# First layer of a two-block model on one Trainium2 core: TensorE's order around the state-space quarters written by hand, attention gate and bias rows moved into it

## Chip, core and metric

The kernel runs on one core of one Trainium2 chip. Five engines each work through a queue of their own: TensorE (PE in the profile, its weight loads PEld), VectorE (DVE), ScalarE (ACT), GpSimd (POOL) and SyncE (SP, which here only issues DMAs). The metric is the device time of one execution in microseconds.

## What is computed

`x` of 1024 tokens by 1024 goes through an even layer (sliding-window attention beside a state-space model), an odd layer (attention over selected tokens) and a second block. The change touches the even layer alone:

```python
def even_layer(hn, rel_bias, w_in, w_out, q_g, k_g, sinks, log_dt, a_re, a_im, b_re, b_im,
               c_re, c_im, d_skip, glu_w, glu_b):
...
    q, k, v, gate_a, u, gate_b = split_cols(hn @ w_in, EVEN_SPLITS)
    q = rms_norm(q.reshape(bsz, L, A_HEADS, A_HEAD_DIM), q_g)
    k = rms_norm(k.reshape(bsz, L, A_KV_HEADS, A_HEAD_DIM), k_g)
...
    att = swa_sink_attention(q, k, v, sinks, rel_bias) * jax.nn.silu(gate_a)
    ssm = s5_mixer(u, log_dt, a_re, a_im, b_re, b_im, c_re, c_im, d_skip, glu_w, glu_b) * jax.nn.silu(gate_b)
    return jnp.concatenate([att, ssm], axis=-1) @ w_out
```

`EVEN_SPLITS` is 512 columns of q, 128 of k, 128 of v, 512 of `gate_a`, 512 of `u` and 512 of `gate_b`. `s5_mixer` projects `u` into 32 groups of 64 complex states, runs a linear recurrence over the tokens, projects back, applies gelu and a gated linear layer.

## The kernel before, in words

**Products.** Every weight product is made in three matmuls (lines 148 to 150): both operands are split into a high and a low part, and high by high, high by low and low by high are added in PSUM. One *step* below is one such group of three. `form1` takes 128 tokens as stationary operand and streams 512 or 256 weight columns; `form2` takes 128 weight columns and streams 512 tokens. A product over the 1024 input features is 8 steps into one PSUM bank of tag `mm`, of which there are 3.

**Weights.** `wpiece` (line 105) loads 128 by 512 from memory (SP's queue), copies it as the high part on ACT (line 122) and subtracts on POOL for the low part (line 123). 13 such tiles fit.

**The first layer, `phase_a` (line 268).** The tokens are normalised and transposed into `hnTA`. Then `bias_rows` makes four small matmuls (`brp`) that turn the position table into rows in memory. The columns `u` are multiplied out (8 banks) and stored. The state-space model works in 4 quarters of 8 groups. `setup(q)` transposes the output table (`craw` to `sg`), forms the tables `w2`, `m3`, `E` on DVE and POOL, multiplies `psG` (stored to `d_g` in 8 DMAs), and transposes `w2` into `m2` through `psm`. All of `sg`, `psG`, `psm` and `brp` use one PSUM bank of tag `sg`. `main(q)` loads its part of `u`, transposes it (`psu`), multiplies by `m2` (`psinc`), and then DVE makes a complex product `z`, eight scans over the tokens and a second complex product `x`. Beside this 16 DMAs load `m1` from `d_g`. `psy` adds `m1` by `u` and `m3` by `x`; DVE copies `y`, `psyT` transposes it, ACT applies gelu.

**Filler.** The products of q (8 banks of 512 columns), of k and v (8 banks of 256) and of `gate_b` (8 banks, `form2`) follow in the program text. A scheduler that works from the dependences and estimated times decides where each instruction stands on its engine; it mixes these products between the quarters' small matmuls. After each bank of q or k, `head_norm` (line 389) squares on ACT, reduces and multiplies on DVE from PSUM into a tile `qo` (tag `qo`, 2 slots, which the bias rows' tiles use too) and stores it to `d_qkv` from SP. After the quarters the PSUM banks are given out anew, and `gate_a` is multiplied out (64 steps), with ACT writing silu of it straight into the tile `mixA`. Then come the gated linear layer `GluA` (which loads `d_gb` into `mixA2`, line 715), the attention `SWA` and the output tiles.

**Names in the rows.** `mm<-w,hnTA` is a product of `form1`, `mm<-hnTA,w` one of `form2`, `mm<-yTs,w` one of the gated linear layer; `zr`, `zi`, `xr`, `xi` are DVE's complex products, `tv` its scratch tile.

## Time and profile before

| what | us |
|---|---|
| median of 3 runs | 2110.9 (2109.47 to 2115.68) |
| the profiled execution, its own time | 2114.89 |
| its span | 2112.6 |

The profiled execution's granted TensorE clock is 0.958 of full speed on average. A row of the timeline gives the start from the beginning of the span, the duration, the engine, the line and the operation; in square brackets stands how long the engine had been idle and what ended this. A row of the stretches gives the stretch, its length, the busy time of PE, PEld, DVE, ACT and POOL (each with its instructions), the granted clock as a share of 2.4 GHz, the busy share of the DMA engines and GB/s. Matmuls overlap in the pipeline, so the time that one costs is read from the distance of two starts.

### The profile page before, as it was taken

Reading aid. Unit: us, or ns where it says so; the run is one execution under the profiler, and the core shown is the slowest. Engines: PE = TensorE matmul, PEld = TensorE weight load, DVE = VectorE, ACT = ScalarE, POOL = GpSimd, SP = SyncE. Lnnn points to the kernel's source line nnn. Section 1 sums busy time; section 2 is a strip of 40 time slices with the busy share of each in tenths; the row PEclk is TensorE's granted clock in tenths of the full one; section 3 lists DMA queues with packets and bytes.
Section 4 is the critical chain, followed back from the end, with each engine's and each line's share of the span. In section 5 each row is a group of like instructions: output and inputs, shape, how many; then the busy total and the mean of one; then the engine's idle time right before and its main releaser. Section 6 shows DMA issues by size and latency. Waiting matters only on the chain. (4 is left out here: it accounts for less than half of the span.)

```text
span 2112.6 us, 27651 instructions
## 1 busy us (share of the span) xinstructions
PE 1938.3 (92%) x9291; PEld 1569.1 (74%) x9291; DVE 1505.6 (71%) x2947; ACT 857.7 (41%) x1740; POOL 920.6 (44%) x774
## 2 busy tenths in 40 slices
PE   7988899989999998899989999999999659999998
PEld 6777777777888876677767788788888537778786
DVE  8375513584469988688856399999997488857737
ACT  5222326564456896555546111223322411134210
POOL 5567416545322247565547221222232586643204
PEclk9989989999999999899999999999999869999999
DMA  6543332313212212643345232223333445575442
GB/s 199 157 121 100 117 125 83 115 49 101 90 56 75 71 46 83 190 171 122 123 150 190 81 103 68 69 90 95 124 118 102 154 136 164 175 243 175 159 160 100
DMA packets 165671, 256.19 MB, mean 121 GB/s; under 512 B 29078, under 2 KB 77548, under 8 KB 165530
## 3 DMA queue, kind: packets, MB, share of 16 engines
q1 hardware_dynamic: 154026, 232.43, 34.6%
q10 hardware_dynamic: 10224, 17.82, 2.3%
q0 software_dynamic: 1280, 4.20, 0.5%
q8 instruction: 73, 1.20, 0.2%
q14 instruction: 68, 0.56, 0.1%
HBM read 185.35 MB, written 75.06 MB: 123 GB/s over the span
## 5 line engine op out<-in xcount | busy, mean ns | idle before, releaser
L123 POOL TENSOR_TENSOR w<-wraw,w 128x512 fp32r<-128x512 f32 (+1 forms) x230 | 312.8, 1374 | 664.6 <-ACT w L122 660.5
L1289 DVE SCALAR_TENSOR_TENSOR cy<-u,cw,cy 128x1024 f32<-128x1024 f32 x232 | 298.7, 1287 | 5.7
L122 ACT ACTIVATE w<-wraw 128x512 fp32r<-128x512 f32 (+1 forms) x230 | 141.2, 623 | 189.6 <-DMA wraw<-in_w_in_dram 47.7
L149 PE MATMUL mm<-hnTC,w 128*128 128x512 f32 (+1 forms) x336 | 131.6, 392 | 0.0
L150 PE MATMUL mm<-hnTC,w 128*128 128x512 f32 (+1 forms) x336 | 131.5, 391 | 0.0
L148 PE MATMUL mm<-hnTC,w 128*128 128x512 f32 (+1 forms) x336 | 131.5, 391 | 0.0
L1167 POOL TENSOR_TENSOR lgB<-lgB,sc 128x1024 f32<-128x1024 f32 (+5 forms) x48 | 84.4, 1791 | 71.7 <-DMA lgB<-d_T 56.6
L148 PE MATMUL mm<-w,ms 128*128 128x512 f32 x256 | 106.0, 414 | 9.7 <-ACT ms L1021 9.3
L150 PE MATMUL mm<-w,ms 128*128 128x512 f32 x256 | 106.5, 416 | 4.3 <-POOL ms L1022 4.2
L1078 ACT ACTIVATE tkj<-sc,tks 128x896 bf16<-128x896 f32 (+2 forms) x93 | 96.7, 1042 | 22.2 <-DVE tks L1074 19.5
L149 PE MATMUL mm<-w,ms 128*128 128x512 f32 x256 | 103.9, 406 | 1.8 <-DVE w L120 1.0
L148 PE MATMUL mm<-w,hnTB 128*128 128x512 f32 x192 | 78.4, 409 | 11.0 <-ACT qo L401 7.7
L148 PE MATMUL mm<-w,hnTA 128*128 128x512 f32 (+1 forms) x192 | 73.4, 386 | 7.6 <-DVE qo L415 7.6
L148 PE MATMUL mm<-hnTB,w 128*128 128x512 f32 (+2 forms) x208 | 79.1, 380 | 0.5 <-DVE wit L872 0.5
L149 PE MATMUL mm<-hnTB,w 128*128 128x512 f32 (+2 forms) x208 | 78.8, 379 | 0.0
L150 PE MATMUL mm<-hnTB,w 128*128 128x512 f32 (+2 forms) x208 | 78.8, 379 | 0.0
L150 PE MATMUL mm<-w,hnTB 128*128 128x512 f32 x192 | 76.9, 400 | 0.0
L149 PE MATMUL mm<-w,hnTB 128*128 128x512 f32 x192 | 76.4, 401 | 0.0
L150 PE MATMUL mm<-w,hnTA 128*128 128x512 f32 (+1 forms) x192 | 73.5, 384 | 0.0
L149 PE MATMUL mm<-w,hnTA 128*128 128x512 f32 (+1 forms) x192 | 72.8, 380 | 0.3 <-POOL w L123 0.3
L148 PEld LDWEIGHTS mm<-hnTC,w 128*128 128x128 f32 (+1 forms) x336 | 61.6, 183 | 14.5
L150 PEld LDWEIGHTS mm<-hnTC,w 128*128 128x128 f32 (+1 forms) x336 | 61.6, 183 | 14.4
(611 smaller groups left out, 5895.1 us busy)
## 6 DMA issues: line engine op xcount, KB each, us to landing
wraw<-in_w_in_dram SPq DMA_DIRECT2D x56, 256.0 KB
wraw<-in_od_w_in_dram SPq DMA_DIRECT2D x48, 256.0 KB
wraw<-in_ev_w_in_dram SPq DMA_DIRECT2D x32, 256.0 KB
wraw<-in_w_in_dram SPq DMA_DIRECT2D x64, 128.0 KB
wraw<-in_w_out_dram SPq DMA_DIRECT2D x32, 256.0 KB
ld<-d_cs SPq DMA_DIRECT2D x16, 512.0 KB
hr<-h SPq DMA_DIRECT2D x24, 256.0 KB
d_T<-d_row SPq DMA_DIRECT2D x8, 576.0 KB
```

The costliest lines, as they stand in the source:

```text
L122: nc.scalar.activation(t[:, 0, :o], raw[:, :o], AF.Copy)
L123: nc.gpsimd.tensor_tensor(t[:, 1, :o], raw[:, :o], t[:, 0, :o].bitcast(F32), op=ALU.subtract)
L148: mm(out, aH, bH, start=start, stop=False)
L149: mm(out, aH, bL, start=False, stop=False)
L150: self.last = mm(out, aL, bH, start=False, stop=stop)
L1078: S.activation(self.junk(n), sc[b], AF.Sign, bias=cand[:, i:i + 1], accum_out=cnt[:, i:i + 1])
L1167: G.tensor_tensor(lg[:, :n], lg[:, :n], self.masks[b], op=ALU.add)
L1289: V.scalar_tensor_tensor(py if i < 30 else y, u[:, i:i + L], cw[:, ct, i:i + 1], py, op0=ALU.mult, op1=ALU.add)
```

## The change

What it does, part by part. (1) TensorE's order around the quarters is written out by hand (`manual_schedule`): `setup` and `main` become generators that stop at fixed places, `filling` yields after every step of q, k and v, `gate_b` and `gate_a` (for k and v after two steps of 256 columns), and `take(n)` issues n of them. In each quarter: 3, `psu`, 4, `psinc`, the next quarter's table transposes and load of `u`, 24, `psy`, 5, `psyT`, 4, `psG` and `psm` of the next quarter. The last call takes what is left. The other engines stay with the scheduler. (2) The bias rows are made one at a time, 4 steps ahead of each. (3) `gate_a` goes into the filler; its silu goes to memory (`d_ga`) in 8 stores of ACT and comes back into `mixA` by 4 loads of 512 KB on SP. (4) `m3` and `E` have 4 slots in place of 3 (two sets). (5) `head_norm` of q, k has ACT copy PSUM into `qo` first and works from there. (6) To make room, the norm's `gb` and `jk` use slots of `m1` and `uT`, and the state-space pools are opened earlier.

```diff
+    def steps1(self, out, hnT, tok0, wt, nk, w):
+
+        for k in range(nk):
+            self.mm3(out, hnT[:, 0, k, tok0:tok0 + P], hnT[:, 1, k, tok0:tok0 + P],
+                     wt[k][:, 0, :w], wt[k][:, 1, :w], k == 0, k == nk - 1)
+            yield
+
+    def steps2(self, out, hnT, tok0, wt, nk, m0):
+
+        for k in range(nk):
+            self.mm3(out, wt[k][:, 0, m0:m0 + P], wt[k][:, 1, m0:m0 + P],
+                     hnT[:, 0, k, tok0:tok0 + 512], hnT[:, 1, k, tok0:tok0 + 512], k == 0, k == nk - 1)
+            yield
+
...
         nc.scalar.dma_start(k.d_row[:, i * 384:(i + 1) * 384], row)
+        yield
...
+    def filling():
         wq = k.wchunk(W, 0, 512)
         for tt in range(NT):
             ps = k.mm()
-            k.form1(ps, hnT, tt * P, wq, KT, 512)
-            head_norm(k, xp, ps, 8, 64, d_qkv[tt * P:(tt + 1) * P, 0:512])
+            yield from k.steps1(ps, hnT, tt * P, wq, KT, 512)
+            head_norm(k, xp, ps, 8, 64, d_qkv[tt * P:(tt + 1) * P, 0:512], 2)
         wkv = k.wchunk(W, 512, 256)
         for tt in range(NT):
             ps = k.mm()
-            k.form1(ps[:, :256], hnT, tt * P, wkv, KT, 256)
+            for i, _ in enumerate(k.steps1(ps[:, :256], hnT, tt * P, wkv, KT, 256)):
+                if i % 2:
+                    yield
             vt = xp.tile([P, 128], F32, tag="vt", name="vt")
             S.activation(vt, ps[:, 128:256], AF.Copy)
             nc.scalar.dma_start(d_qkv[tt * P:(tt + 1) * P, 640:768], vt)
-            head_norm(k, xp, ps[:, :128], 2, 64, d_qkv[tt * P:(tt + 1) * P, 512:640])
-        wg = k.wchunk(W, 1792, 512)
-        for m in range(4):
-            for th in range(2):
-                ps = k.mm()
-                k.form2(ps, hnT, th * 512, wg, KT, m * P)
-                gt = xp.tile([P, 512], F32, tag="gt", name="gt", bufs=2)
-                S.activation(gt, ps, AF.Silu)
-                nc.scalar.dma_start(d_gb[m * P:(m + 1) * P, th * 512:th * 512 + 512], gt)
+            head_norm(k, xp, ps[:, :128], 2, 64, d_qkv[tt * P:(tt + 1) * P, 512:640], 2)
+        for c0, dst in ((1792, d_gb), (768, d_ga)):
+            wg = k.wchunk(W, c0, 512)
+            for m in range(4):
+                for th in range(2):
+                    ps = k.mm()
+                    yield from k.steps2(ps, hnT, th * 512, wg, KT, m * P)
+                    gt = xp.tile([P, 512], F32, tag="gt", name="gt", bufs=2)
+                    S.activation(gt, ps, AF.Silu)
+                    nc.scalar.dma_start(dst[m * P:(m + 1) * P, th * 512:th * 512 + 512], gt)
+    fill = filling()
+    def take(n):
+        for _ in range(n):
+            next(fill, None)
+    ss = SSM(k, sp, tl, xp, d_u, d_y, d_g)
+    with tc.manual_schedule(engines={mybir.EngineType.PE}):
+        rows = bias_rows(k, xp)
+        runs = [ss.main(q) for q in range(4)]
+        prep = ss.setup(0)
+        next(prep)
+        next(runs[0])
+        for _ in range(4):
+            take(4)
+            next(rows)
+        next(prep)
+        for q in range(4):
+            take(3)
+            next(runs[q])
+            take(4)
+            next(runs[q])
+            if q < 3:
+                prep = ss.setup(q + 1)
+                next(prep)
+                next(runs[q + 1])
+            take(24)
+            next(runs[q])
+            take(5)
+            next(runs[q], None)
+            if q < 3:
+                take(4)
+                next(prep)
+            if q == 1:
+                for h in range(8):
+                    bias_spread(k, d_sw, h, 0, 384)
+        take(500)
+    sS.close()
...
         gl = GluA(k, c2, d_y, d_gb, mix2)
-        wg = k.wchunk(W, 768, 512)
         for m in range(4):
-            for th in range(2):
-                ps = k.mm()
-                k.form2(ps, hnT, th * 512, wg, KT, m * P)
-                S.activation(mix[:, m, th * 512:th * 512 + 512], ps, AF.Silu)
+            nc.sync.dma_start(mix[:, m], d_ga[m * P:(m + 1) * P, :])
...
-    if leave:
+    if leave == 2:
+        S.activation(o, ps, AF.Copy)
+        ps = o
+    elif leave:
...
-        m3 = [t512("m3", "m3r", 3), t512("m3", "m3i", 3)]
+        m3 = [t512("m3", "m3r", 4), t512("m3", "m3i", 4)]
...
-        er, ei = t512("E", "er", 3), t512("E", "ei", 3)
+        er, ei = t512("E", "er", 4), t512("E", "ei", 4)
```

PE around the second quarter's state products, before (`psinc` is the input product, `psy` the output, `mm` rows are filler):

```order
L634 MATMUL psinc<-uTa,m2r 64x128 x4
L634 MATMUL psinc<-uTa,m2i 64x128 x4
L634 MATMUL psinc<-uTb,m2r 64x128 x4
L634 MATMUL psinc<-uTb,m2i 64x128 x4
L660 MATMUL psy_1162<-m1a,uTa 128x128 x2
L660 MATMUL psy_1162<-m1b,uTb 128x128 x2
L660 MATMUL psy_1163<-m1a,uTa 128x128 x2
L660 MATMUL psy_1163<-m1b,uTb 128x128 x2
L148 MATMUL mm<-w,hnTA 128x256
L149 MATMUL mm<-w,hnTA 128x256
```

and in the changed kernel:

```order
L693 MATMUL psinc<-uTa,m2r 64x128 x4
L693 MATMUL psinc<-uTb,m2r 64x128 x4
L693 MATMUL psinc<-uTa,m2i 64x128 x4
L693 MATMUL psinc<-uTb,m2i 64x128 x4
L610 MATMUL sg<-ident,craw 128x64 x2
L148 MATMUL mm<-w,hnTA 128x512
L149 MATMUL mm<-w,hnTA 128x512
L150 MATMUL mm<-w,hnTA 128x512
L148 MATMUL mm<-w,hnTA 128x256
```

The output product's first matmuls stood right behind the input product; now 3 matmuls of 512 and 138 of 256 columns stand between (in the other quarters 72 of 512).

PE where `psG` ends and `psm` follows (the `sg` bank), in the changed kernel, ahead of the second quarter:

```order
L639 MATMUL psG<-cbd,w2r 128x32
L639 MATMUL psG<-cbd,w2i 128x32
L654 MATMUL psm_1348<-ident,w2r 128x128 x4
L654 MATMUL psm_1354<-ident,w2i 128x128 x4
L148 MATMUL mm<-w,hnTA 128x512
L149 MATMUL mm<-w,hnTA 128x512
L150 MATMUL mm<-w,hnTA 128x512
```

Before, filler stood between the three: in the first two quarters 11 and 21 matmuls between `psG` and the first `psm`, and over 20 between the two `psm`. Now all three stand together.

SP's queue behind the quarters, before (`yf`, `mixA_2588`, `qkv` feed the gated linear layer and the attention, `wraw` the output weights):

```order
L704 DMA yf<-d_y 128x512 x2
L715 DMA mixA_2588<-d_gb 128x512 x7
L704 DMA yf<-d_y 128x512
L715 DMA mixA_2588<-d_gb 128x512
L704 DMA yf<-d_y 128x512
L750 DMA qkv<-d_qkv 128x768 x2
L704 DMA yf<-d_y 128x512 x2
L110 DMA wraw<-in_ev_w_out_dram 128x512 x3
```

and in the changed kernel:

```order
L765 DMA yf<-d_y 128x512 x2
L811 DMA qkv<-d_qkv 128x768 x2
L765 DMA yf<-d_y 128x512 x4
L110 DMA wraw<-in_ev_w_out_dram 128x512 x3
L1087 DMA xr<-in_x_dram 128x512 x2
L110 DMA wraw<-in_ev_w_out_dram 128x512
L413 DMA mixA<-d_ga 128x1024 x4
L110 DMA wraw<-in_ev_w_out_dram 128x512
L776 DMA mixA_2874<-d_gb 128x512 x2
```

All loads of `mixA_2874` moved behind the first output weights, the four new loads of `mixA` stand ahead of them, and the third `qkv` load comes behind all of them (the piece ends at the first two `mixA_2874`).

## Rows read from the trace of the kernel before

**Rows 1.** Three stretches: length, busy us (count) of five engines, clock, DMA share, GB/s.

```profile
67.40:321.50 254.10, 223.25 (x1268) 184.78 (x1267) 110.31 (x186) 66.61 (x110) 131.59 (x117) 0.91 0.43 127
200.00:240.00 40.00, 40.00 (x247) 32.62 (x246) 17.68 (x30) 15.48 (x20) 23.04 (x22) 1.00 0.47 136
280.00:294.00 14.00, 14.00 (x61) 10.77 (x60) 0.39 (x3) 5.19 (x8) 5.11 (x4) 1.00 0.84 297
```

**Rows 2.** Waits of 60 to 330 us: us in total, times, longest.

```profile
PE psy L666 <- DVE xr L425: 9.4, 1, 9.4
...
PE mm L148 <- DVE qo L415: 7.6, 3, 4.0
...
DVE qo L415 <- DMA d_qkv<-qo: 5.7, 2, 4.5
...
PE psy L660 <- DMA m1a<-d_g: 5.5, 1, 5.5
```

**Rows 3.** PE, timeline: pairs of `form1` 512, `form1` 256 and `form2` matmuls.

```profile
92.67 0.40 PE L149 MATMUL mm<-w,hnTA 128*128 128x512 f32 x1
...
99.32 0.39 PE L148 MATMUL mm<-w,hnTA 128*128 128x512 f32 x1
...
193.30 0.28 PE L148 MATMUL mm<-w,hnTA 128*128 128x256 f32 x1
...
196.01 0.28 PE L150 MATMUL mm<-w,hnTA 128*128 128x256 f32 x1
...
318.71 0.39 PE L148 MATMUL mm<-hnTA,w 128*128 128x512 f32 x1
...
321.51 0.39 PE L148 MATMUL mm<-yTs,w 128*128 128x512 f32 x1
```

**Rows 4.** PE, groups of 200 to 240 us: busy us, mean ns, idle before.

```profile
L149 PE MATMUL mm<-hnTA,w 128*128 128x512 f32 x42 | 16.7, 402 | 0.0
```

**Rows 5.** PE, timeline: products of the position rows.

```profile
77.19 0.80 PE L225 MATMUL brp<-oh,rb 33*8 33x384 f32 x2
...
85.18 0.80 PE L225 MATMUL brp<-oh,rb 33*8 33x384 f32 x2 [1.12 <-DMA oh<-in_c_oh_dram]
```

**Rows 6.** PE and ACT, timeline: transpose and copy of `m2`.

```profile
106.16 0.60 PE L598 MATMUL psm<-ident,w2r 128*128 128x128 f32 x4
...
106.80 0.60 ACT L599 ACTIVATE m2r<-psm 128x512 f32<-128x512 f32 x1 [0.75 <-PE psm L598]
```

**Rows 7.** PE, timeline: 256-column matmuls behind the second `psG`.

```profile
188.91 0.41 PE L148 MATMUL mm<-w,hnTA 128*128 128x256 f32 x1
...
191.47 0.41 PE L148 MATMUL mm<-w,hnTA 128*128 128x256 f32 x1
```

**Rows 8.** DVE, timeline: chain of quarter 0 (first pair), 2 (three rows), 3 (three rows).

```profile
115.61 0.69 DVE L423 TENSOR_TENSOR zr<-psinc,er 128x512 f32<-128x512 f32 x1
...
136.84 1.49 DVE L428 TENSOR_TENSOR xi<-xi,tv 128x508 f32<-128x508 f32 x1
...
211.05 0.69 DVE L423 TENSOR_TENSOR zr<-psinc,er 128x512 f32<-128x512 f32 x1 [8.05 <-PE psinc L634]
...
215.59 1.56 DVE L642 TENSOR_TENSOR_SCAN zr<-smalls,zr 128x128 f32<-128x128 f32 x4
...
223.36 0.69 DVE L428 TENSOR_TENSOR xi<-xi,tv 128x508 f32<-128x508 f32 x1
...
249.53 0.69 DVE L423 TENSOR_TENSOR zr<-psinc,er 128x512 f32<-128x512 f32 x1 [19.63 <-PE psinc L634]
...
252.92 4.34 DVE L642 TENSOR_TENSOR_SCAN zr<-smalls,zr 128x128 f32<-128x128 f32 x4
...
267.69 0.69 DVE L428 TENSOR_TENSOR xi<-xi,tv 128x508 f32<-128x508 f32 x1
```

**Rows 9.** SP and PE, timeline: gate loads; use of the third `qkv` load.

```profile
280.05 3.47 SPq L715 DMA_DIRECT2D mixA<-d_gb  x7
...
347.72 0.62 PE L764 MATMUL tq<-ident,qkv 128*128 128x128 f32 x4
```

More of the change, by code (lines that the diff above doesn't have):

```diff
@@ L228, in bias_rows, with rms_hn @@
         nc.scalar.dma_start(k.d_row[:, i * 384:(i + 1) * 384], row)
+        yield
 def bias_spread(k, dst, h, c0, n):
     k.nc.sync.dma_start(dst[h], dap(k.d_row, h * 1536 + c0, [[0, P], [1, n]]))
-def rms_hn(k, pool, hnT, xt, gb, ms, rs, tt, tag="tp", halves=0):
+def rms_hn(k, pool, hnT, xt, gb, ms, rs, tt, tag="tp", halves=0, jk=None):
     V, S = k.nc.vector, k.nc.scalar
-    jk = pool.tile([P, D], BF16, tag="jk", name="jk", bufs=1)
+    if jk is None:
+        jk = pool.tile([P, D], BF16, tag="jk", name="jk", bufs=1)
     if halves:
@@ L249, in rms_hn @@
     k.rstd(rs[:, tt:tt + 1], ms[:, tt:tt + 1])
-    for h in range(1 + halves):
-        n = D // (1 + halves)
+    two = isinstance(gb, list)
+    for h in range(1 + two):
+        n = D // (1 + two)
         hs = slice(h * n, h * n + n)
-        V.scalar_tensor_tensor(xt[:, hs], xt[:, hs], rs[:, tt:tt + 1], gb[:, hs], op0=ALU.mult, op1=ALU.mult)
+        V.scalar_tensor_tensor(xt[:, hs], xt[:, hs], rs[:, tt:tt + 1], gb[h] if two else gb, op0=ALU.mult, op1=ALU.mult)
     k.to_hnT(xt, hnT, tt, tag)
@@ L278, in phase_a @@
     d_gb = tc.dram_tile([512, L], F32, name="d_gb")
+    d_ga = tc.dram_tile([512, L], F32, name="d_ga")
     d_sw = tc.dram_tile([8, P, 384], F32, name="d_sw")
@@ L284, in phase_a @@
     hnT = hp.tile([P, 2, KT, L], F32R, name="hnTA")
-    gb = smp.tile([P, D], F32, name="gbA")
     ms = smp.tile([P, 8], F32, name="msA")
     rs = smp.tile([P, 8], F32, name="rsA")
+    sS = ExitStack()
+    sp, tl = [sS.enter_context(k.pool(n)) for n in ("ssm_s", "ssm_t")]
+    gb = [tl.tile([P, 512], F32, tag="m1", name="gbA", bufs=2) for _ in range(2)]
+    jk = tl.tile([P, 512], F32, tag="uT", name="jkA", bufs=2).bitcast(BF16)
     xts = []
@@ L294, in phase_a @@
                 nc.scalar.dma_start(xt[:, 512:], x[0:P, 512:])
-                k.bcast_row(gb, ins["norm_g"][0], D)
+                for h in range(2):
+                    nc.sync.dma_start(gb[h], dap(ins["norm_g"][0], h * 512, [[0, P], [1, 512]]))
             else:
@@ L305, in phase_a @@
             nc.sync.dma_start(xt, x[tt * P:(tt + 1) * P, :])
-        rms_hn(k, xp, hnT, xt, gb, ms, rs, tt, ("tp", "sg"), 1 if tt==0 else 0)
-    bias_rows(k, xp)
+        rms_hn(k, xp, hnT, xt, gb, ms, rs, tt, ("tp", "sg"), 1 if tt==0 else 0, jk)
     for tt in range(NT):
@@ L313, in phase_a @@
         nc.sync.dma_start(d_u[tt * P:(tt + 1) * P, :], ut)
-    with ExitStack() as c1:
-        ss = SSM(k, c1, xp, d_u, d_y, d_g)
-        for q in range(4):
-            ss.setup(q)
-            ss.main(q)
-        for h in range(8):
-            bias_spread(k, d_sw, h, 0, 384)
+    def filling():
         wq = k.wchunk(W, 0, 512)
@@ L431, with __init__ @@
 class SSM:
-    def __init__(self, k, cx, xp, d_u, d_y, d_g):
-        self.k, self.xp, self.d_u, self.d_y, self.d_g = k, xp, d_u, d_y, d_g
+    def __init__(self, k, sp, tl, xp, d_u, d_y, d_g):
+        self.k, self.sp, self.tl, self.xp, self.d_u, self.d_y, self.d_g = k, sp, tl, xp, d_u, d_y, d_g
         nc, ins = k.nc, k.ins
         V, S, G, T = nc.vector, nc.scalar, nc.gpsimd, nc.tensor
-        self.sp = sp = cx.enter_context(k.pool("ssm_s"))
-        self.tl = cx.enter_context(k.pool("ssm_t"))
         raw = sp.tile([16, 3, P], F32, name="raw")
@@ L578, in setup @@
              v4(t512("tg", "tg", 1)), conj_b=True)
+        yield
         ps = k.ps("sg", "psG")
@@ L606, in setup @@
         self.par[q] = m2, m3, er, ei
+        yield
     def main(self, q):
@@ L612, in main @@
         t512 = self.t512
-        m2, m3, er, ei = self.par.pop(q)
         j0 = q * 4
@@ L620, in main @@
         S.activation(ug.rearrange("c g t h -> c t g h"), uq.rearrange("c t (g h) -> c t g h", g=8), AF.Copy)
+        yield
+        m2, m3, er, ei = self.par.pop(q)
         uT = [t512("uT", "uTa", 2), t512("uT", "uTb", 2)]
@@ L627, in main @@
             S.activation(uT[hf], ps, AF.Copy)
+        yield
         uTg = lambda g: uT[g // 4][:, (g % 4) * P:(g % 4 + 1) * P]
@@ L655, in main @@
                     dap(d_g, (q * P + hf * 64) * 240 + (7 - t) * 16, [[240, 16], [240 * 16, 4], [1, P]]))
+        yield
         y = big("y").rearrange("c (t h) -> c t h", t=8)
@@ L670, in main @@
                           psy[par].rearrange("c (j t h) -> c t j h", j=4, t=8))
+        yield
         yT = big("yT")
```

## The prediction

> **What bounds the kernel now.** I read three views, in this order. First the stretches of the first layer. The products of `u` end at about 67.4 us and the last matmul of `gate_a` is followed by the first of the gated linear layer at 321.5. In these 254.1 us TensorE is busy for 223.25 at a mean clock of 0.91 [rows 1]. It is therefore idle for 30.85 us, and part of its busy time goes at the lower level of 1.2 GHz. Between 200 and 240 us it has neither: busy for all 40 us at full clock [rows 1]. So PE is the bound of this stage, and what can be won is idle time and slow clock, no work.
>
> Second the waits. The three longest of PE's are 9.4 us on DVE's `x` in the last quarter, 5.5 us on the `m1` load in the first, and 7.6 us (3 times) on the multiplication into `qo` that still holds a product's PSUM bank [rows 2].
>
> Third the timeline, for the price of a matmul at full clock: 512 columns of `form1` (99.32 - 92.67) / 29 = 0.229 us, 256 columns (196.01 - 193.30) / 23 = 0.118, `form2` (321.51 - 318.71) / 12 = 0.233 [rows 3]. Behind the second `psG`, in which PE had waited, 256 columns cost (191.47 - 188.91) / 12 = 0.213 [rows 7]: nearly twice as much, the lower level of the clock.
>
> From these prices, the stage without a wait. Left at 67.4 us are 192 matmuls for q (44.0 us), 192 of 256 columns for k and v (22.7), 384 for both gates (89.5), three bias products of 0.8 (2.4) [rows 5], and the quarters' own matmuls. The stretch of 200 to 240 us holds one quarter's set and 42 steps of `gate_b` [rows 4]: 40 - 42 x 3 x 0.233 = 10.6 us for a quarter, 42.4 for four. The sum is 201, so the ideal end is 268.4, and before loses 53 us: 31 idle, 22 to the clock. In this stage one us of waiting cost another 0.72 us of slow clock, and I price every new wait at 1.72.
>
> **The change, part by part.** *Removed.* With 24 steps (72 matmuls, 16.5 to 16.8 us, for k and v 138 of 256 columns, 16.3) between `psinc` and `psy`, DVE's `z`, scans and `x` and the `m1` loads of the same quarter run beside filler. The last quarter gets filler that it did not have, because 64 steps of `gate_a` now come ahead of the PSUM change; 172 of 224 steps are taken by the quarters, and 52 (156 matmuls, 36.4 us) stay behind the last `psyT`. The work is the same, so what is won is the 53 us less what the fixed order still waits for. As PE works its queue in order, all filler behind a wait stands too.
>
> *Bias rows.* `brp` 1, 2 and 3 now come after 4 steps each (2.75 us of filler, 3.6 with the product itself). Each needs a table load into a `qo` slot that is free, and a copy and a store in between; the slots are shared with the first two banks of q. Before, two of them stood 8.0 us apart, the second after a wait of 1.12 on its load [rows 5]. If 8.0 is the chain's own length, three waits of 4.4 follow, 13 us; if the schedule set it, nothing. I take 5, nearer the lower end, because the wait shown is only 1.12.
>
> *The one `sg` bank.* `psG`, `psm`, `psm` now follow each other without filler, and each needs the bank of the one before: a copy by DVE, then one by ACT. The `m2` transposes end about 106.75, ACT's copy of 0.60 ends at 107.4 [rows 6]; that is 0.9 us of idle PE with the handover, and with the shorter copy of `psG` (taken as half) about 1.4 for a quarter, 5.6 for four. Bounds: 3.6, as the second `psm` cannot pass ACT's copy, and 7.2 if both copies cost 0.9.
>
> *Products of k and v.* ACT now copies a bank into `qo` at once, so the 7.6 us of waits for DVE [rows 2] lose their first cause. But `qo` has two slots, each free only when DVE has multiplied and the store has landed. DVE is in the `x` chain of quarter 1 when the first banks of k come, and its multiplication of the last q bank stands behind that. The bank then waits for `qo` in place of DVE; the three PSUM banks cover 2 products of 2.8 us. Bounds: 0 and 7.6 + 5.7 = 13.3, the waits of before with the store's own [rows 2]. I take 5.5, the length of such a chain of one store (up to 4.5 [rows 2]) and a multiplication. In all other products DVE and ACT have 5.5 us for a bank and are hidden.
>
> *DVE's chain against its cover.* From the first product to the end of `xi` it took 22.7 us in quarter 0, 13.0 in quarter 2 and 18.9 in quarter 3 [rows 8]. Against a cover of 16.5 to 16.8 us quarter 2's length is hidden, the other two are not. In quarter 3 the four scans took 4.34 us beside POOL's weight conversions, against 1.56 in quarter 2 [rows 8]. Which chains meet POOL's conversions and tables is not fixed by the text. Bounds: 0 and 6.2 + 2.1 = 8.3. I take 1, since in quarter 3 part of POOL's conversions are now done earlier, and quarter 0's chain had other work in its midst. The Trainium skill, page "SBUF — State Buffer", section "Who interferes with whom", says that a DVE instruction with two SBUF inputs contends with a GpSimd instruction that reads SBUF. By that rule every chain with POOL at work beside it would be a long one, and the time would be that of the second rival below; the trace agrees on the scans of quarter 3 and disagrees on those of quarter 2, where POOL was busy for 23.04 of 40 us [rows 1].
>
> *Copies, tables.* ACT's 16 copies (0.6 or less each), 8 silu stores of 256 KB and the fourth slots of `m3` and `E` cost nothing: ACT is busy for 66.6 of 254 us [rows 1], and `take` gives it 5.5 us for a bank.
>
> *Sum of the stage.* Waits of 5 + 5.6 + 5.5 + 1 = 17.1 us, with the clock 29.4. The stage ends at 268.4 + 29.4 = 297.8 in place of 321.5: 23.7 us won.
>
> *Behind the stage.* Before, `mixA_2588` was loaded at 280 us, under `gate_a` [rows 9], when 14 us moved 297 GB/s [rows 1]. Now these 2 MB and another 2 MB of `d_ga` wait for the last silu's store and for the old tiles' room, so they start about 3 us behind the last `gate_a` matmul, and SP has the third `qkv` load behind them. 4.2 MB at 297 GB/s are 14 us. Before, PE first used that `qkv` 26.2 us after the stage's end (347.72) [rows 9]. 3 + 14 and the load, its copy and transposes come close to that. Bounds: 0, and 8 with the slower clock. I take 3.5 lost.
>
> So 23.7 - 3.5 = 20.2 us are won against the profiled execution, 2114.9 to 2094.7. That execution is 4.0 above the median of 2110.9, so the **forecast is 2090.7 us**. Later stages have no changed text, and I put them at no difference. About 0.3% (6.3 us) is what a measurement of this kernel can tell from no change.
>
> **The rivals.** *Few waits.* The bias loads land in time, `qo` is free, the chains fit: only the `sg` bank is left, 5.6 x 1.72 = 9.6, the stage wins 43.4, less 3.5 behind it: 2071. For it speaks that quarter 2 ran without any wait [rows 1]; against it that the three places share slots which I can name.
>
> *No change: the chains stay as long as with POOL beside them.* POOL has the next quarter's tables and the gates' conversions to make while the chains run, and DVE may lose its turns to it in every quarter as it did in quarter 3. Three chains of 18.9 and the first of 22.7 [rows 8] against their covers give 2.1 x 3 + 6.2 = 12.5 us of waits in place of 1; 11.5 x 1.72 = 19.8 us less won, so about 2110. Against it: quarter 2 had POOL work too and took 13.0 [rows 8]. That all chains stay long is what the Trainium skill's page "SBUF — State Buffer", section "Who interferes with whom", would lead one to expect.
>
> *Slower: each quarter like quarter 0.* If DVE's queue has `head_norm` work and waits in the midst of the chain, as in quarter 0, each takes 22.7 us. PE then stands 24 us in `psy` with no filler that it could take instead: 23 x 1.72 = 40 us less won, 20 slower: 2130. The point from which it decides: the 20.2 us are used up by 11.7 us of added wait, that is chains of about 19.7 us in every quarter. For it: filler products and chain share DVE. Against it: quarters 2 and 3, 13.0 and 18.9, of which only one is near.
>
> *The order does nothing*, because the other engines keep their old limits: then 2111. Against it: the largest waits of PE are of its own order (`psy` right behind `psinc`, nothing left for the last quarter).
>
> **Numbers.** Forecast with its bounds, 2080 to 2104: 0.67. Few waits: 0.15. No change in either form: 0.10. Slower: 0.08. The range of 2070 to 2106 leaves out the better part of the slower cases and the best of the few-waits case. Faster by over 0.3%: 0.83, within: 0.09, slower: 0.08.
>
> **What would show it.** In the changed profile the last `gate_a` matmul should end near 298 us. PE's waits of `psy` on `xr` and on `m1a` should be gone or under 2 us; new ones should stand at `brp` (on the table load or the row copy), at the second `psm` (on ACT's copy), and at the k products (on ACT's `qo` copy, and behind that the store). Behind the stage PE should wait for `qkv` or its transposes. I am wrong if `psy` still waits for `xr` for several us in most quarters, if the clock of the stage stays at 0.91, or if the stage gains and later stages give it back.

## The result: slower by 0.6%, and the profile after

The changed kernel takes 2125.2 us (median of 6 runs, 2115.85 to 2129.19) against 2111.7 in 6 runs of before: a ratio of 1.0057, interval 1.0037 to 1.0078. The forecast was 2090.7, with slower at 0.08. The profiled execution took 2117.96 us, 7 below its median. To separate the stage from what lies around it I use three marks in each trace: the end of the products of `u`, the first matmul of the gated linear layer (*stage end*) and the first product of the next layer (`mm<-hnTB`).

| us | before | forecast | after |
|---|---|---|---|
| start to the end of `u`'s products | 67.4 | as before | 70.5 |
| stage, from there to its end | 254.1 | 230.4 | 254.1 |
| stage end to next layer | 220.7 | 224.2 | 230.1 |
| next layer to end of span | 1570.4 | as before | 1561.5 |

The stage should have become 24 us shorter and stayed as long as it was; behind it 9 us were lost in place of 3.5. The rest has no changed text; in the profiled executions of all sixteen kernels told of here it lies between 1561.5 and 1577.0 us, so several us of a total are not the stage's. In the same sixteen the products of `u` end between 67.2 and 73.6 us; *own_rows* below has the 67.2 with the text of these products as in after, so I do not put the 3.1 us to the change. In after the first entry of the hand order stands right behind them:

```profile
70.48 0.34 PE L610 MATMUL sg<-ident,craw 64*128 64x64 f32 x2
```

The stretches of after (length; busy us and count of PE, PEld, DVE, ACT, POOL; clock; DMA share; GB/s), to hold against [rows 1]; the first begins at 67.4 like the one there, so it has 3.1 us of `u` in it, in which PE was not idle:

```profile
67.40:324.62 257.22, 220.62 (x1280) 182.41 (x1278) 113.18 (x184) 74.85 (x128) 133.24 (x120) 0.91 0.42 125
80.00:100.00 20.00, 11.41 (x38) 7.67 (x36) 4.01 (x8) 5.22 (x8) 13.78 (x12) 0.74 0.60 170
140.00:160.00 20.00, 13.57 (x67) 11.58 (x68) 7.82 (x14) 10.26 (x15) 10.73 (x12) 0.74 0.37 111
180.00:200.00 20.00, 11.18 (x97) 10.94 (x98) 15.96 (x27) 2.52 (x9) 13.99 (x14) 0.70 0.10 34
324.62:554.70 230.08, 210.20 (x1002) 167.59 (x1002) 126.89 (x332) 130.56 (x309) 120.08 (x150) 0.95 0.32 104
```

Idle is 257.2 - 220.6 = 36.6 us in place of 30.85, at the same clock of 0.91, which was one of the signs of being wrong that the prediction named. Idle time is bunched: three stretches of 20 us hold 23.8 us of it. PE's waits of 60 to 330 us (total, times, longest), which replace those of [rows 2]:

```profile
PE mm L148 <- ACT qo L455: 12.8, 1, 12.8
...
PE psyT L736 <- DVE y L729: 8.2, 1, 8.2
PE brp L239 <- DMA oh<-in_c_oh_dram: 7.9, 2, 6.5
...
PE psm L654 <- ACT m2r L655: 4.9, 4, 2.9
```

The waits of `psy` on `xr` and on `m1a`, 14.9 us before, are gone, as the change intends. With 2.1 us of `psm` on `gs` and 0.7 of `psG` on the last row, 12.8 + 8.2 + 7.9 + 4.9 + 2.1 + 0.7 is the whole 36.6. So the order did its work, and four waits that had been small or absent before (`brp` 1.1 us, `y` 2.0) took more than it gave.

**Where they come from.** *Bias rows.* The timeline, PE then ACT:

```profile
87.70 1.44 PE L239 MATMUL brp<-oh,rb 33*8 33x384 f32 x2 [6.52 <-DMA oh<-in_c_oh_dram]
...
90.51 0.63 PE L148 MATMUL mm<-w,hnTA 128*128 128x512 f32 x1
90.94 0.63 PE L149 MATMUL mm<-w,hnTA 128*128 128x512 f32 x1
...
95.18 0.80 PE L239 MATMUL brp<-oh,rb 33*8 33x384 f32 x2 [1.34 <-DMA oh<-in_c_oh_dram]
```

```profile
81.03 0.58 ACT L455 ACTIVATE qo<-mm 128x512 f32<-128x512 f32 x1
...
82.89 0.30 ACTq L237 DMA_DIRECT2D oh<-in_c_oh_dram  x1
...
96.01 0.60 ACT L455 ACTIVATE qo<-mm 128x512 f32<-128x512 f32 x1 [9.45 <-PE brp L239]
```

The third product's table load goes out only at 82.89. A bank of q has one of the two `qo` slots from 81.03 on; the other has to take the first row, the second row, whose copy on DVE waited 4.70 us for the first row's store, and only then this table, which takes until 87.6 to land. Behind the wait a matmul of 512 columns costs 0.43 us (90.94 - 90.51) in place of 0.229 [rows 3]: the lower level of the clock. And the second bank of q waits 9.45 us in turn for the rows to leave its slot.

*`y` of quarter 0.* SP, ACT, then DVE:

```profile
130.88 8.41 SPq L474 DMA_DIRECT2D d_qkv<-qo  x2
139.38 0.39 SPq L602 DMA_DIRECT2D braw<-in_ev_ssm_b_re_dram  x1
```

```profile
135.43 0.60 ACT L455 ACTIVATE qo<-mm 128x512 f32<-128x512 f32 x1 [14.86 <-DMA d_qkv<-qo]
```

```profile
136.72 0.69 DVE L469 TENSOR_REDUCE hm<-sq 128x8 f32<-128x512 f32 x1 [4.68 <-ACT sq L468]
...
139.12 0.23 DVE L484 TENSOR_TENSOR tb<-braw,smalls 128x64 f32<-128x64 f32 x1
...
141.95 0.22 DVE L481 TENSOR_TENSOR tb<-braw,smalls 128x64 f32<-128x64 f32 x1 [2.35 <-DMA braw<-in_ev_ssm_b_im_dram]
...
143.85 1.27 DVE L729 COPY y<-psy 128x512 f32<-128x512 f32 x2
```

`psy` is finished at 133.4, and the copy of `y`, which PE needs, comes at 143.85. DVE works its queue in order, and ahead of this copy stand table work of the last two quarters and two banks of q. DVE stands still there twice. The first time, 4.68 us, it waits until ACT has squared a bank of q, whose copy got a `qo` slot only at 135.43, when a store had landed. The second time, 2.35 us, it waits for small loads of the last quarter's `braw`. They leave SP at 139.38, behind two stores of `qo`; but `braw` has one slot, and DVE's last read of the tile before it (139.12) ends at 139.35, so which of the two held them cannot be read here. The rest of the delay is DVE's own work. Slots and a queue that works in order make one wait of 8.2 us for PE.

*First k banks.* DVE's chain of quarter 1, then ACT:

```profile
162.75 0.69 DVE L480 TENSOR_TENSOR zr<-psinc,er 128x512 f32<-128x512 f32 x1 [5.70 <-PE psinc L693]
...
166.80 1.90 DVE L701 TENSOR_TENSOR_SCAN zr<-smalls,zr 128x128 f32<-128x128 f32 x4
...
173.46 4.24 DVE L701 TENSOR_TENSOR_SCAN zi<-smalls,zi 128x128 f32<-128x128 f32 x4
...
181.46 1.47 DVE L485 TENSOR_TENSOR xi<-xi,tv 128x508 f32<-128x508 f32 x1
...
184.60 1.75 DVE L472 TENSOR_TENSOR qo<-qo,hr 128x512 f32<-128x512 f32 x1
```

```profile
188.49 0.28 ACT L455 ACTIVATE qo<-mm 128x128 f32<-128x128 f32 x1 [12.13 <-DVE w2i L485]
```

The chain takes 162.75 to 182.93, 20.2 us, and the last q bank's multiplication stands behind it at 184.60. Until it is stored (the store goes out at 186.37), one of two `qo` slots is taken; k banks follow at half the distance of q banks, all three PSUM banks fill, and PE waits 12.8 us. The releaser that ACT's row names, `w2i`, is only the last thing that DVE ended before 188.49; the copy does not read it. *Behind the stage*, SP's queue, against [rows 9]:

```profile
330.46 1.75 SPq L413 DMA_DIRECT2D mixA<-d_ga  x4
...
336.83 4.60 SPq L776 DMA_DIRECT2D mixA<-d_gb  x5
342.01 0.32 SPq L811 DMA_DIRECT2D qkv<-d_qkv  x1
```

The gates' loads start 6 us behind the stage's end, and the third `qkv` comes behind them all. But `qkv` has two slots, and this load follows PE's last read of the first tile, a transpose that starts at 341.00; in before it follows the same transpose (334.15) at 334.78. So it is not seen to wait for the gates' loads.

### The profile page after: what moved, and what is told of

It is laid out like the page before. It is cut to its first block, busy times and chain, and to the rows that moved or that the text cites. A ratio compares the mean times of both kernels' runs of the same rounds, so it can differ in the third digit from the quotient of the medians.

```text
span 2116.2 us, 27727 instructions
## 1 busy us (share of the span) xinstructions
PE 1935.4 (91%) x9291; PEld 1565.5 (74%) x9291; DVE 1508.5 (71%) x2954; ACT 865.7 (41%) x1756; POOL 921.6 (44%) x774
## 5 line engine op out<-in xcount | busy, mean ns | idle before, releaser
L123 POOL TENSOR_TENSOR w<-wraw,w 128x512 fp32r<-128x512 f32 (+1 forms) x230 | 307.7, 1353 | 673.1 <-ACT w L122 665.7
L148 PE MATMUL mm<-w,hnTA 128*128 128x512 f32 (+1 forms) x192 | 73.7, 387 | 12.8 <-ACT qo L455 12.8
L148 PEld LDWEIGHTS mm<-hnTC,w 128*128 128x128 f32 (+1 forms) x336 | 61.6, 183 | 14.6
L149 PEld LDWEIGHTS mm<-hnTC,w 128*128 128x128 f32 (+1 forms) x336 | 61.6, 183 | 14.4
L150 PEld LDWEIGHTS mm<-hnTC,w 128*128 128x128 f32 (+1 forms) x336 | 61.6, 183 | 14.3
L149 PE MATMUL mm<-w,hnTA 128*128 128x512 f32 (+1 forms) x192 | 72.1, 377 | 0.1
```

The lines of the kernel that those rows point to most:

```text
L123: nc.gpsimd.tensor_tensor(t[:, 1, :o], raw[:, :o], t[:, 0, :o].bitcast(F32), op=ALU.subtract)
L148: mm(out, aH, bH, start=start, stop=False)
L149: mm(out, aH, bL, start=False, stop=False)
L150: self.last = mm(out, aL, bH, start=False, stop=stop)
```

## The experiments

Ratios are to before, with 95% intervals; every edit is made to the changed kernel unless it says otherwise. A stage's length is counted from the end of `u`'s products in the run itself, and its idle time is PE's; where an expectation names an end, that is the time from the start of the execution, and the scatter of `u`'s end is in it.

### Bias rows: whose slots, or which place?

*own_rows*: the rows' two tiles out of the `qo` slots, into slots of the state-space pool.

```diff
-        oh = p.tile([33, 384], F32, tag="qo", name="oh", bufs=2)
+        oh = p.tile([33, 384], F32, tag="z", name="oh", bufs=2)
...
-        row = p.tile([8, 384], F32, tag="qo", name="brow", bufs=2)
+        row = p.tile([8, 384], F32, tag="x", name="brow", bufs=2)
...
-        rows = bias_rows(k, xp)
+        rows = bias_rows(k, tl)
```

> The changed kernel with the bias rows' tiles (table load, row) in slots of z and x, which nothing uses yet, and no longer in the two qo slots. Slots theory: PE's waits ahead of brp (6.5 + 1.3 us, and 0.7 at the first psG) go, with the slow clock from 88 to 107 us that follows them: the first psinc comes 9 to 14 us earlier than 110.6, the stage ends 5 to 14 us earlier than 324.6, since the later qo waits may take part back. Rival (the order of SP or of ACT's queue sets when the tables land): brp still waits over 4 us, and the stage ends within 3 us of 324.6.

Measured: 2100.8 us, 0.9933 (0.9921 to 0.9945). The four products now stand without a wait, 3.7 to 3.8 us apart:

```profile
74.08 0.81 PE L239 MATMUL brp<-oh,rb 33*8 33x384 f32 x2
77.78 0.81 PE L239 MATMUL brp<-oh,rb 33*8 33x384 f32 x2
81.62 0.80 PE L239 MATMUL brp<-oh,rb 33*8 33x384 f32 x2
```

The stage is 242.1 us long, 12.0 less than in after, with 23.8 us idle in place of 36.6; its end, 309.2, is a little earlier than expected. Behind it the stretch takes 222.7, 7.4 less. PE's k wait fell with it from 12.8 to 9.6 and that on `y` from 8.2 to 5.0; new are 2.4 us of `psG` behind POOL's work on weights. Which slots the rows use decides the sign of the change.

*qo3*: a third `qo` slot instead (`bufs=3`), rows still in them. *rows_qo3*: both.

> The changed kernel with a third qo slot (2 KB that are free), bias rows still in them. Slots theory: the 8.2 us of psyT on y in the first quarter and the 12.8 us of the k products on ACT's qo copy shrink to under 4 us each, brp's waits to under half; the stage ends 15 to 30 us before 324.6. Rival (DVE's x chain and SP's order, not the number of slots): the slots only move the wait by one bank, 2.8 us for k and 5.5 us for q, and the stage ends 3 to 10 us earlier.

> Both of the above: bias rows out of qo, and three qo slots. Slots theory: none of the three waits is over 3 us, the stage ends near 290 to 298 us (27 to 35 us before 324.6), and the whole execution is 15 to 30 us faster than the kernel before. Rival (waits of the chain itself): at least one wait of over 6 us of psy or psyT on DVE's x or y takes their place, the stage ends after 305, and the execution is within 10 us of the kernel before.

Measured: 2103.4, 0.9953 (0.9939 to 0.9968), and 2099.5, 0.9923 (0.991 to 0.9936); stages of 237.4 and 237.3 us, idle 23.2 and 21.9. By the ratios a third slot does about what own slots do, and both do hardly more than one: it is one cause. The wait on `y` is 3.8 us in both, but k banks still wait 9.5 and 7.8, where under 4 and under 3 were expected.

*rows_first*: the four rows ahead of the products of `u`, as before, slots shared.

```diff
+    for _ in bias_rows(k, xp):
+        pass
     for tt in range(NT):
...
-        rows = bias_rows(k, xp)
...
             take(4)
-            next(rows)
```

> The changed kernel with one part undone: the four bias rows are made ahead of the products of u, as before, and not between the steps of q; two qo slots as in the change. Slots theory: PE's 8.6 us of waits around brp and psG go, as they did when the rows had slots of their own (2100.8 us, ratio 0.993), so 0.992 to 0.996 here. Rival (a later wait takes them back as the qo slots stay the same for q and k): 0.998 to 1.005.

Measured: 2119.3, 1.0041 (1.002 to 1.0061), in the rival's range and not to be told from after's ratio; the stage is 250.9 us long, idle 33.8. But no later wait took the gain back, as the rival had it: PE still waits for the tables, 6.9 us against 7.9.

```profile
78.94 1.44 PE L239 MATMUL brp<-oh,rb 33*8 33x384 f32 x2 [4.78 <-DMA oh<-in_c_oh_dram]
82.48 1.44 PE L239 MATMUL brp<-oh,rb 33*8 33x384 f32 x2 [2.10 <-DMA oh<-in_c_oh_dram]
```

The scheduler put the four products at 67.8 to 82.5 us (in after 73.7 to 95.2), and the first bank of q comes to its slot at 92.4. So even with no bank of q between them, table, row and next table go through two slots one after the other. The rows' place alone is not the cause.

### The one `sg` bank

*sg_two*: the first `m2` transposes into another PSUM bank. *three*: this, with *rows_qo3*.

```diff
-            ps = k.ps("sg", "psm2")
+            ps = k.ps("sg" if i else "tp", "psm2")
```

> The changed kernel with the first m2 transpose in the PSUM bank of the norm's transposes (unused by then) in place of the sg bank. The sum of idle PE at psG and psm is 7 us in the changed kernel (0.4 + 0.7, 0.6 + 0.7, 0.7 + 2.9, 0.4 + 0.7). If these waits are on the path they go, but for what comes behind: the stage ends 4 to 9 us before 324.6. If the qo slots set the pace, what is won here is waited for there: under 3 us.

> The changed kernel with bias rows out of qo, three qo slots and the first m2 transpose in the other PSUM bank. Alone, the first two ended the stage at 306.5 us and the third at 316.1, against 324.6. If waits at psG and psm are on the path even where qo does not wait (7.6 us are left there with rows and slots mended), the stage ends near 296 to 300 and the execution is 5 to 10 us faster than with rows and slots alone (ratio to before 0.987 to 0.990). If they are hidden by what waits later: 303 to 307, ratio 0.991 to 0.993.

Measured: *sg_two* 2115.3, 1.0008 (0.9997 to 1.0019); of the waits of `psm`, 7.0 us, 0.3 are left, and `psy` has new ones of 4.1. The stage is 243.5 us long, 10.6 less, its end 316.1 as expected. *three*: 2097.8, 0.9922 (0.9905 to 0.9939), a stage of 229.1 us, end at 297.6. The end is the expected one; the ratio is not, since the stretch behind took 228.7 us. That is about the forecast's stage (230.4), with the k wait still at 9.5.

### The first k banks

*copy_only*: the kernel before with nothing but part 5, ACT's copy.

```diff
-    if leave:
+    if leave == 2:
+        S.activation(o, ps, AF.Copy)
+        ps = o
+    elif leave:
```

> The kernel before with one part of the change alone: ACT copies a product's bank into qo first, and square and multiplication read the copy. If the PSUM bank held by DVE's multiplication was what stopped PE in the kernel before (7.6 us in three waits, with the slow clock 13), those waits go and the execution is 5 to 13 us faster than before. If the two qo slots take its place (the copy needs a free slot, which the multiplication alone did as well), within 4 us of before.

Measured: 2112.1, 0.9994 (0.9979 to 1.0009). PE waits 1.3 us for banks of k in place of 7.6 [rows 2], but `psy` on `xr` now 12.3 us in place of 9.4 and `psu` 4.9: what one wait gave up, others took. Alone the copy neither gains nor harms.

*gb_no_low*: POOL writes zeros in place of the low part of `gate_b`'s weights (the product of `gate_b` then lacks the part with the weights' low half). POOL's eight subtractions for it are gone.

```diff
-                nc.gpsimd.tensor_tensor(t[:, 1, :o], raw[:, :o], t[:, 0, :o].bitcast(F32), op=ALU.subtract)
+                if low:
+                    nc.gpsimd.tensor_tensor(t[:, 1, :o], raw[:, :o], t[:, 0, :o].bitcast(F32), op=ALU.subtract)
+                else:
+                    nc.gpsimd.memset(t[:, 1, :o].bitcast(F32), 0.0)
...
-            wg = k.wchunk(W, c0, 512)
+            wg = k.wchunk(W, c0, 512, low=c0 != 1792)
```

> The changed kernel in which POOL writes zeros for the low part of gate_b's weights in place of the subtraction (this leaves out the low part of gate_b's weights; loads, matmuls and the number of POOL instructions stay). In the changed kernel DVE's chain of the second quarter, from the first product to the end of xi, takes 20.2 us, and its scans run beside POOL's eight subtractions. Contention theory: without them the chain takes 13 to 16 us, and the k products' wait shrinks from 12.8 to 6 to 9 us. Slots theory alone: chain and wait stay within 1.5 us, as the wait hangs on the multiplication of the last q bank and the order of DVE's queue.

Measured: 2115.7, 1.001 (0.9987 to 1.0032); chain 18.1 us and k wait 3.5, so neither expectation is met. DVE and POOL in quarter 1 (this kernel's lines stand 3 higher than after's):

```profile
165.45 0.69 DVE L483 TENSOR_TENSOR zr<-psinc,er 128x512 f32<-128x512 f32 x1 [7.65 <-PE psinc L696]
...
175.02 1.35 DVE L704 TENSOR_TENSOR_SCAN zi<-smalls,zi 128x128 f32<-128x128 f32 x4
...
178.21 1.60 DVE L475 TENSOR_TENSOR qo<-qo,hr 128x512 f32<-128x512 f32 x1
...
181.67 1.85 DVE L488 TENSOR_TENSOR xi<-xi,tv 128x508 f32<-128x508 f32 x1
```

```profile
174.99 2.66 POOL L185 TENSOR_TENSOR hr<-hm,mhalf 128x8 f32<-128x8 f32 x2 [0.71 <-DVE hm L473]
```

and POOL beside the second four scans of after:

```profile
173.28 1.11 POOL L483 TENSOR_TENSOR m3i<-cT,pw 128x512 f32<-128x512 f32 x1
174.36 1.41 POOL L123 TENSOR_TENSOR w<-wraw,w 128x512 fp32r<-128x512 f32 x1
175.73 1.38 POOL L482 TENSOR_TENSOR m3r<-m3r,tg 128x512 f32<-128x512 f32 x1
```

The second four scans take 1.35 us in place of 4.24. Beside the 4.24 stand two table entries of POOL and only one of the eight subtractions, beside the 1.35 only POOL's small `hr`. So it is not the subtractions alone that stretch the scans, but POOL's work on 128 by 512 of either kind. The chain is only 2.1 us shorter (165.45 to 183.52), as POOL's tables now run beside its other parts; the first four scans take 2.55 us in place of 1.90. PE's k wait falls from 12.8 to 3.5 while the scheduler also puts the q multiplication ahead of the chain's end, 12.8 us behind `zr` in place of 21.9. How much each of the two is worth, this run does not separate. The Trainium skill, page "SBUF — State Buffer", section "Who interferes with whom", says that DVE and GpSimd contend for a pair of SBUF ports that they share, one locking the other out. The scans agree, 4.24 us against 1.35.

*k_own*: *own_rows* and *sg_two*, and copies and squares of k in slots of their own.

```diff
-        o = pool.tile([P, 512], F32, tag="qo", name="qo", bufs=2)[:, :n]
+        o = pool.tile([P, 128], F32, tag="ko", name="ko", bufs=3) if leave == 2 and nh == 2 else pool.tile([P, 512], F32, tag="qo", name="qo", bufs=2)[:, :n]
...
-    sq = pool.tile([P, 512], F32, tag="sq", name="sq", bufs=1)
+    sq = pool.tile([P, 128], F32, tag="ksq", name="ksq", bufs=2) if leave == 2 and nh == 2 else pool.tile([P, 512], F32, tag="sq", name="sq", bufs=1)
```

> As the one before, but qo has two slots, and the k products have three small slots for their copy and two for their squares (2.5 KB in all). Slots theory: PE's wait of the k products (12.8 us in the changed kernel, 7.8 with three qo slots) goes to under 3 us, and the y wait of the first quarter stays at 4 to 8. Rival (DVE's x chain of the second quarter, 19.7 us beside POOL's weight conversions, with the k work behind it in DVE's order): the k products still wait 4 us or more, with DVE's reduction or multiplication as the releaser.

Measured: 2099.7, 0.993 (0.9914 to 0.9946). The k wait falls to 3.0 us, from 9.5 in *three*, so slots are its cause; the stage is 231.9 us, no shorter than that of *three* (229.1), since 6.6 us of waits on `y` (3.8 in *three*) and 4.4 of `psm` on `gs` stand in its place.

*kv_last*: *three*, with the filler in the order q, `gate_b`, `gate_a`, k and v.

> Bias rows out of qo, three qo slots, the first m2 transpose in the other bank, and the filler's order changed: q, both gates, then k and v last (32 of their steps and the end of the gates stand behind the last psyT). Then no k bank meets DVE's chain. If the k wait (9.5 us in the same kernel with k second, stage end 297.6) and its slow clock are what is left of the loss, the stage ends near 283 to 290 us. Behind it the attention waits for the last k and v stores: the stretch behind is 225 to 235 against 228.7. The execution: 5 to 12 us faster than that kernel's 2097.8. Rival: DVE's chain beside POOL now makes psy itself wait, over 4 us in two or more quarters, and the stage ends after 293.

Measured: 2094.0, 0.9916 (0.9895 to 0.9937). No k wait is left, but the stage is 231.5 us long and ends at 300.2, against the expected 283 to 290: `psyT` waits 10.1 us for `y` (3.8 in *three*) and `psy` 3.7 for `xi`, less than the rival asked for.

### The gate back behind the quarters

*gate_back*: `gate_a` as before, straight into `mixA`, no store and no load.

> The changed kernel with the attention gate back behind the quarters, silu straight into mixA, as before; the hand order then runs out of filler in the last quarter. Late-loads theory: behind the stage nothing is lost (from its end to the first product of the next layer 219 to 222 us, as before with 220.7, against 230.1), and in the last quarter psy waits up to 10 us. Net with the changed kernel within 6 us either way. Rival (what was lost behind the stage was not the loads): that stretch stays at 226 to 231.

Measured: 2123.3, 1.0042 (1.0029 to 1.0055). The two stretches:

```profile
67.40:336.40 269.00, 228.26 (x1290) 187.84 (x1289) 115.84 (x187) 76.57 (x131) 134.78 (x119) 0.90 0.41 121
336.40:554.00 217.60, 200.58 (x1002) 161.95 (x1001) 125.04 (x329) 130.86 (x309) 120.88 (x150) 0.98 0.28 90
```

Counted from the end of `u` (72.4) the stage takes 264.0 us. Against after, 12.5 us are won behind the stage and 9.9 lost in it, which is within the 6 us expected. The loss does not lie where it was expected: `psy` does not wait in the last quarter. Idle time is 4.1 us more, with one new wait of 4.2 for a small load (`gr`), and the rest is busy time. Nor does this run show what late loads cost: in the twelve other kernels with these loads the second stretch took 222.7 to 228.7 us, in before 220.7. *own_rows*, with 222.7, has the four loads of `mixA` 6.5 us behind its stage's end and the third `qkv` at 18.7, later than after (5.8 and 17.4).

### What makes `y` late, and all mends together

*braw_pool*: the two small loads issued by POOL. *best* and *best2*: rows in own slots, *sg_two*, k's own slots and this, in the order of *kv_last* and in that of the change.

```diff
-            nc.sync.dma_start(bb[:, i], ins[a][0][2 * j0:2 * j0 + 8].rearrange("(j g) p h -> (g p) j h", g=2))
+            nc.gpsimd.dma_start(bb[:, i], ins[a][0][2 * j0:2 * j0 + 8].rearrange("(j g) p h -> (g p) j h", g=2))
```

> The changed kernel, with the two small loads of braw issued by POOL in place of SP; nothing else. Theory: psyT waited 8.2 us for y because SP stood 8.4 us at the store of qo (130.9 to 139.3), the braw loads came behind that store, and DVE, working in order, stood at the table product of braw ahead of the copy of y. Then the wait of psyT on y falls under 3 us, and the stage ends some 8 to 14 us sooner than 324.6 (8.2 less what is left, at up to 1.72), unless another of DVE's entries is as late; ratio to before 0.998 to 1.003. Rival: DVE is late for y because of its own load (head_norm on qo, whose store holds the slot); then psyT still waits 5 us or more for y, and the stage ends within 3 us of 324.6.

> All mends in one: bias rows out of the qo slots, first m2 transpose in the other PSUM bank, k's own copy slots, braw loads on POOL, and the order of the filler q, gate_b, gate_a, k and v. Theory: the waits removed one by one add up; in the stage only psy on the chain and 2 to 4 us for psm and psG are left: it ends at 283 to 293, and the total is 0.987 to 0.991 of before. Rival: DVE and SP, now the late ones, move the wait to psyT or psy as they did in the run with k and v last; the stage ends at 295 to 302 and the total is 0.991 to 0.994.

> The same mends in the filler order of the change (q, k and v, gate_b, gate_a). Theory: against the run with rows, bank and k's own slots (stage end 300.7) only the wait of psyT on y (4.5 and 2.1) goes, which gives an end at 289 to 296 and 0.988 to 0.992 of before. Rival: y is late for another reason, and the end stays within 3 us of 300.7, 0.991 to 0.994.

Measured for *braw_pool*: 2119.7, 1.0014 (0.9997 to 1.003). The wait on `y` falls from 8.2 to 4.2 us, between the two expectations; the stage is 251.6 us long, 2.5 less, idle 32.9, and ends at 325.2, within the rival's 3 us, as `u` ends 3.1 later. POOL, then DVE:

```profile
140.22 0.82 POOL L602 DMA_DIRECT2D braw<-in_ev_ssm_b_re_dram  x1 [1.51 <-DVE fb L485]
```

```profile
143.31 0.23 DVE L481 TENSOR_TENSOR tb<-braw,smalls 128x64 f32<-128x64 f32 x1 [0.18 <-DMA braw<-in_ev_ssm_b_im_dram]
143.46 1.28 DVE L729 COPY y<-psy 128x512 f32<-128x512 f32 x2
```

Free of SP's queue, the load still goes out only when DVE has done with the tile before it, at 140.22. So SP's queue is not shown as a cause of the wait. DVE's order is another here: its last product for `w2i` (135.66) stands ahead of the entry that waited for the square in after, and DVE has no gap over 0.2 us. Half of the wait is left: DVE works without a longer gap up to the copy, and the load lands only just before it, so either would hold `y` there.

*best*: 2102.4, 0.9937 (0.992 to 0.9955); the stage is 231.7 us long and ends at 304.2, later than both expectations, `psyT` on `y` 15.2 us. *best2*: 2091.3 (2089.55 to 2099.78), 0.9893 (0.9874 to 0.9912), the fastest of all. Its stretches and waits:

```profile
67.40:300.30 232.90, 217.83 (x1285) 181.70 (x1283) 123.07 (x184) 75.10 (x130) 135.18 (x122) 0.96 0.46 138
300.30:523.00 222.70, 203.76 (x1002) 163.38 (x1003) 126.64 (x332) 130.77 (x308) 120.30 (x150) 0.98 0.33 108
```

```profile
PE psyT L736 <- DVE y L729: 6.5, 2, 3.8
```

Idle is 15.1 us, `mm<-hnTB` starts at 523.0. The only edit against *k_own* is the loads' queue. The wait on `y` is 6.5 us against 6.6, so the rival was right: `y` is late for another reason, and the end, 300.3, is within 3 us of 300.7. Counted from the end of `u` (71.9) the stage is 228.5 us, 3.4 shorter; what went is chiefly the wait of `psm` on `gs`, 4.4 us there and 0.3 here. That its median is 8 us lower comes in part from behind `mm<-hnTB` or from the scatter of runs, and stays open. In the order of *kv_last* the same mends give less; which of DVE's entries delay `y` there was not followed further.

## Why the prediction was wrong, by its own steps

**The ideal and the bound held.** PE bounds the stage, and idle time and slow clock were what there was to win. The waits to be removed were removed. The mended kernels have stages of 229.1 us (*three*) and 228.5 (*best2*), the forecast said 230.4; *best2* has 2091.3 us, the forecast 2090.7. That the numbers meet is in part luck: *three* is idle for 17.0 us, as forecast (17.1), but 9.5 of them are the k wait, taken at 5.5, and 3.8 the wait on `y`, which the sum did not have. The forecast describes a kernel in which the shared slots cost little; the change is not that kernel.

**Bias rows: the step that decided.** I took 5 us out of 0 to 13, "nearer the lower end, because the wait shown is only 1.12" [rows 5]. The idle time was 8.6 us, within the bounds. What was mis-sized is its reach: with the clock and the q banks that wait for the same slots, undoing it takes 12.8 us of idle time and 12.0 us of length from the stage, and 24 us from the median (2125.2 to 2100.8); in the profiles another 7.4 us lie behind the stage, from a cause that is not shown. The 1.12 us of before had been measured with no bank of q in those slots; I named the sharing and priced the rows alone.

**k and v: 5.5 taken, 12.8 measured**, near the upper bound of 13.3. I had the mechanism (two slots, a multiplication behind the chain of quarter 1) and took the length of one store and one multiplication, where the wait lasts as long as what is left of the chain.

**`sg` bank: 5.6 taken, 7.0 measured**, the upper bound being 7.2; undone, it gives 10 us (2125.2 to 2115.3).

**Chain against its cover: 1 taken, 0 measured at `psy`, by two errors that cancelled.** I gave long chains little chance because quarter 2 "had POOL work too", 23.04 us in 40 [rows 1]. That is an average over 40 us. During the scans of that quarter, from 215.59 [rows 8] to 219.61, POOL stood idle but for their first 0.3 us:

```profile
214.48 1.44 POOL L427 TENSOR_TENSOR tg<-cT,pw 128x512 f32<-128x512 f32 x1
...
221.01 1.78 POOL L426 TENSOR_TENSOR ei<-lo,hi 128x512 f32<-128x512 f32 x1 [5.09 <-DVE xi L426]
```

So the trace did not speak against that rival, nor against the rule that was cited with it. In after the chains take 17.0, 20.2, 20.3 and 12.5 us. PE does not wait for them because the cover is longer than my 16.5 to 16.8: from the chain's first product to the first product of `psy` that reads `x` it is 19.5 us in quarters 0 and 3, 19.8 in quarter 2 and 34.4 in quarter 1, since the products with `m1` and transposes stand there too and, in quarter 1, the k wait. The long chain of quarter 1 did its harm at another place: it held the q multiplication, and so the k banks.

**A term that was missing: `y`, 8.2 us.** I asked who waits on each queue for the edits one by one, and not what stands ahead of the copy of `y` on DVE. This step failed outright. About half of it hangs on the same two slots (5.0 us with the rows out of them, 3.8 with a third); the rest is DVE's order, and which entries of it was not settled.

**Sum.** The four terms and `y` account for the idle time: 17.1 forecast, + 3.6 rows, + 1.4 bank, + 7.3 k, + 7.2 for `y` less the chain's 1 = 36.6. The factor of 1.72 was too high for after: 201 us of work, the fourth bias product (0.8) and 36.6 idle leave 15.7 us of the stage's 254.1 to the clock, 0.43 for each, not 0.72; in *own_rows* it is (242.1 - 201.8 - 23.8) / 23.8 = 0.69.

**Behind the stage: 3.5 taken, 9.4 measured** in after, outside the bounds of 0 to 8; 2.0 in *own_rows* and *best2*, 8.0 in *three*. The gates' loads are late as said, but PE nowhere waits for `qkv`, as I had it. I had also taken PE's use of the second `qkv` (347.72 [rows 9]) for that of the third, which before transposes only at 358.69, 37.2 us behind its stage's end, and after 40.9 behind its own. What fits late loads are its waits on `sg`, 4.7 us in place of 2.9. Most of the 9.4 is busy time, 210.2 us in place of 203.3 at a clock of 0.95 in place of 0.97; why is not shown.

**Chances.** Four of five terms came out at or above what I took. The waits at the rows, at k and at `y` are not independent: all hang on two `qo` slots and on DVE's queue, and a bank that is late through one makes the next late. My range treated the terms as if they would even out. No rival had this case.

## What to carry to other kernels

Before an order is fixed by hand on the engine that bounds, list for each thing it waits for the tile slots and the in-order queues that it shares with others, and price the longest way through them with all the sharers in it; waits that vanish in one place can come back at another. Small tiles that a DMA fills and another DMA empties belong in slots of their own, not in those of the stream that feeds the bound engine. When several uncertain terms share a resource, add their upper ends together as one case and give it a chance. To say that two engines ran side by side, read the few us in question, not an average over a longer stretch.

## What was not expected of the hardware

The same four scans of 128 by 128 took 1.35 or 1.36 us undisturbed, 4.24 in quarter 1 of after beside two table entries and a subtraction of POOL, and four times the 1.36 where tables ran without a gap. DVE and POOL in quarter 2 of *best2*:

```profile
206.77 5.56 DVE L701 TENSOR_TENSOR_SCAN zi<-smalls,zi 128x128 f32<-128x128 f32 x4
```

```profile
206.27 1.72 POOL L482 TENSOR_TENSOR m3r<-m3r,tg 128x512 f32<-128x512 f32 x1
...
210.63 1.42 POOL L481 TENSOR_TENSOR tg<-lo,hi 128x512 f32<-128x512 f32 x1
```

In after the clock was low where PE had stood: 0.70 to 0.74 in the three stretches of 20 us with long waits, against 0.91 over the stage.
